# A decoder layer in one kernel: pacing of accumulating DMAs, new places for the next block's input, and 32-wide score products

## The chip, the cores and the metric

The kernel runs on one core of a Trainium2 chip. The metric is the device time of one launch in microseconds (us), the median of three runs. One further execution was taken by the hardware profiler; every duration below is from that one.

The names of the profile: PE is TensorE (matmuls), PEld its weight loads, DVE is VectorE, ACT is ScalarE, POOL is GpSimd, SP is SyncE, which here only issues DMAs. L12 is line 12 of the kernel before. In the changed kernel the lines stand a little lower: by 1 from L119, by 5 from L349, by 10 behind the scores and by 12 in FF2.

## What is computed

One inference step of a hybrid decoder layer, in float32, for one prompt of 2048 tokens and for 8 sequences of 8 sample tokens. Cut to what matters:

```python
proj = einsum('btd,dp->btp', x, w_in)                 # 1024 -> 3584
q, f_pre, i_val, g, gate_b, gate_c, h = split(proj)
qh, f, kh, vh = silu(q), gate(f_pre), 1 - f, i_val    # 4 heads of 128
S_t = diag(f_t) S_{t-1} + k_t outer v_t               # per head, 128x128
o_t = S_t^T q_t
o = rmsnorm(o) * onorm_g * silu(g)
yc = gate_b * conv3(gate_c * h)                       # causal, width 3
x = layer_norm(ALPHA * x + concat(o, yc) @ w_out)
hid = square(relu(x @ w_ff1))                         # 1024 -> 4096
x = layer_norm(ALPHA * x + hid @ w_ff2)               # 4096 -> 1024
```

The results are x for all tokens, the final states S, and the last two rows of the convolution's input.

## The kernel before

**Blocks and phases.** The prompt is worked in four blocks b = 0..3 of 512 tokens; block 1 carries the 64 sample tokens as well. A block has a phase m (the projections m1, m2, m3, the recurrence beside them, then the products with w_out) and a phase f (LayerNorm, FF1, FF2). The hidden width of 4096 falls into 8 chunks c of 512. The chunks come in two parts of four; each part runs its FF1 and then its FF2.

**Products.** A float32 product is three matmuls of rounded pieces: high by high, high by low, low by high (`mm3` L236 to L239, `mm3_on` L241 to L245, and `mm_pair` L247 for the sample tokens). So every operand is split in two: ACT writes the high piece, DVE subtracts it from the original and writes the low piece (`split` L161, where ACT's line is L162 and DVE's L163).

**Units of weights.** All weights, and the input x too, pass as a list of "units", each 128x1024 (512 KB). SP loads a unit into `st` (L180, three buffers); ACT makes `wh` (L201) and DVE `wl` (L208), four buffers each. `weights(i)` (L224) hands out unit i, and before that `ahead` (L215) issues the loads and splits up to three units further on. A unit of x has its own function: it splits `st` into the tile X (again L162 and L163). Since each engine works strictly in order, the place of a unit in the list is the place of its split in ACT's and DVE's queues, and of its load in SP's.

**Where the next block's x stands in the list.** While the list is built (L383), the units of x for block b+1 are put among the FF2 units of part 1: `X_PLACES` (L49) names the FF2 steps and the chunks after which the next one goes in. There are four such units, and a fifth one for the sample tokens before block 1.

**FF2 and FF1 by seven products.** FF2 of a part, and FF1 from chunk 2 on in blocks 1 to 3, use a scheme in the manner of Strassen: seven products (`PRODUCTS`, in the order T4, B11, B21, T2, T1, T3, B22) of sums of quarters in place of eight plain ones. Each FF2 step goes over the part's four chunks, 28 units of 12 matmuls (128x512) each. Before a unit `prepare` (L1197) splits a quarter of the hidden values into h (ACT L162) and l (DVE L163), three buffers each; it runs two units ahead, since the last two FF1 units each call it once. `sum_rows` (L1221) makes sums of hidden values on DVE, and at a step's end `add_to` (L1229) adds the step's two PSUM banks into the output tiles: two additions for some steps, four for T3.

**Sums of the weights.** The sums T1 to T4 of the quarters of w_ff2 (`T_b`) and of w_ff1 (`T_a`) are made once, in device memory, by DMAs that POOL issues: per chunk eight, half of them with an accumulating write (`make_sums` L340, issued at L345 and L347). The generator `making` makes the 64 for w_ff2 while block 0 is in its phase m, and `making1` the 48 for w_ff1 (chunks 2 to 7). In block 0's FF1, which is plain because T_a is not there yet, three `making1` steps follow each unit of part 0 and two each unit of part 1: 8 units of part 0 and 16 of part 1, so the 48 are used up by part 1. T_a is first read in block 1's FF1.

**The recurrence.** For a head (`head`, L564 to L698) the scores of 128 tokens by 128 tokens are put together by levels: on level `lev` the tokens are paired in neighbouring groups of L = 2^lev, keys from the one and queries from the other, and after each level `decay` multiplies the gates into q and k for the next. Levels 0 and 1 are sums made with a matrix of ones. On levels 2 to 6 PE multiplies keys by queries, for each of the four groups of 128 tokens of a block (L677). Level 4 and below use one product of 128x128 per group, level 5 two of 32x32, level 6 one of 64x64. On levels 2 to 4 DVE then takes the valid places out of PSUM by one predicated copy of 128 partitions by 256 elements (`place`, L597); on levels 5 and 6 there are plain copies of rectangles (L680). The steps of this generator are called between the units of m1, m2 and m3, so one level's matmuls stand as a short burst among the projections on PE, and its copies between the weight splits on DVE.

**Temporary tiles.** In phase f, `TMP` (L92) takes its tile from the three buffers tagged "h", which FF2's h uses too.

Of the kernel before, what the change touches and what calls it, by code (L numbers as in the profile page):

```python
# [9 lines left out]
F32 = mybir.dt.float32  # L10
# [3 lines left out]
ALU = mybir.AluOpType  # L14
# [31 lines left out]

SAMPLE = {"B21": (1, ((0, 1),)), "B11": (0, ((0, 1), (1, -1))), "T1": (0, ((1, 1),)), "B22": (1, ((1, 1),))}

X_PLACES = (("T3", 4), ("T3", 6), ("B22", 4), ("B22", 5), ("B22", 6))  # L49

QUARTER = {"B11": (0, 0), "B21": (1, 0), "B12": (0, 1), "B22": (1, 1)}

# [8 lines left out]
def hybrid_step(ctx, tc, a, o):  # L61
# [27 lines left out]

    def TMP():  # L90

        return S((P, 4, P)) if phase["in"] == "m" else new((P, 4, P), "h", 3, F32, phase["of"])  # L92

    def TOK(dt=F32):
        return new((P, D), "tok", 8, dt)
# [20 lines left out]
    small = cst.tile([P, 36], F32, name="small")  # L116
    lnb = cst.tile([P, 2, D], F32, name="lnb")
    nhalf = cst.tile([P, NH], F32, name="nhalf")
    halo = cst.tile([P, 4, 2], F32, name="halo")  # L119
    lw = cst.tile([P, 6, NH], F32, name="lw")  # L120
    lbl, onorm, convw = small[:, 0:4], small[:, 4:8], small[:, 8:20]
# [218 lines left out]
    def make_sums(at, cs):  # L340
        for to, of, acc in (("T1", "B11", False), ("T3", "B22", False), ("T1", "B12", True), ("T3", "B12", True),
                            ("T2", "T3", False), ("T2", "B11", True), ("T4", "T2", False), ("T4", "B21", True)):
            for c in cs:
                if acc:
                    g.dma_start(at(c, to), at(c, of), accum_op=ALU.add, max_dma_last_dim=4096)  # L345
                else:
                    g.dma_start(at(c, to), at(c, of), max_dma_last_dim=4096)  # L347
                yield

    making = make_sums(quarter2, range(NCH))  # L350
    making1 = make_sums(quarter1, range(NPLAIN, NCH))
# [46 lines left out]
    for b in range(NB):  # L398
# [165 lines left out]
        def head(h):  # L564
# [106 lines left out]
            for lev in range(2, 7):  # L671
                ps = PS((P, NC, P))
                L = 1 << lev
                for c in range(NC):

                    for x, y, w in (((0, 0, P),), ((0, 32, 32), (64, 96, 32)), ((0, 64, 64),))[max(lev - 4, 0)]:
                        te.matmul(ps[x:x + w, c, y:y + w], k3[:, c, x:x + w], q3[:, c, y:y + w], start=True, stop=True)  # L677
                if lev > 4:
                    for x in range(0, P, 2 * L):
                        v.tensor_copy(sc[x:x + L, :, x + L:x + 2 * L], ps[x:x + L, :, x + L:x + 2 * L])  # L680
                else:
                    place(lev, L, pairs(ps.rearrange("p c t -> p (c t)"), L)[:, :, 1, :])
                sample_scores(lev)
                decay(lev)
                yield
# [165 lines left out]
        for i, _ in enumerate(main()):  # L851
            rec_step()
            if b == 0 and i >= 6:
                if i == 6:

                    g.tensor_tensor(SM((P, 1)), ks[0][:, 0:1], fs[0][:, 0:1], ALU.add)
                next(making, 0)
                next(making, 0)
            if i >= 16 and i % (3 if samp else 4) == 0:
                rec_step()  # L860
            if i % 2 == 0:
                pump()
# [383 lines left out]
        for part, (ff1_units, ff2_units) in enumerate(pl["parts"]):  # L1246
            queue += [(step, c) for step, c, _ in ff2_units]
            for i, (step, c, u) in enumerate(ff1_units):
                if i >= len(ff1_units) - 2:
                    prepare()  # L1250
                if b == 0:
                    if i == 0:
                        for _ in making:
                            pass
                    ff1(step, weights(u), segs)
                    for _ in range(3 - part):
                        next(making1, 0)
                else:
                    ff1_product(step, c, weights(u))
            drain()  # L1260
# [19 lines left out]
            for n_, (step, c, u) in enumerate(ff2_units):  # L1280
# [15 lines left out]
                if first:  # L1296
                    banks[k] = [PS() for _ in range(2)]
                h, l = hid.pop((step, c))
                for p in range(2):
                    cs = slice(p * P, p * P + P)  # L1300
                    for q, (rh, rl) in enumerate(parts):
# [151 lines left out]
```

## Time and profile before

| | |
|---|---|
| median of three runs | 2425.33 us (2424.86 to 2428.46) |
| the profiled execution: its time | 2427.2 us |
| its span, first to last instruction | 2425.4 us |
| mean granted clock of PE | 0.993 |
| PE busy | 2369.6 us, 98% |
| DVE, ACT, POOL busy | 71%, 50%, 7% |
| moved by DMA | 412.40 MB, 170 GB/s on average |
| `T_b` and `T_a` DMAs of POOL, issue to landing (median) | 18 to 24 us |
| loads of `st` by SP, issue to landing (median) | 3.5 to 4.5 us |

A line of waits reads "engine tile line <- engine tile line that released it: us in all, times, longest". A line of the timeline reads "start, duration, engine, line, operation, tiles, shape, count", and in brackets the idle time before it and what ended it. A group of instructions reads "line engine op out<-in count | busy us, mean ns of one | idle before, releaser". "L245 <- l" is a matmul that waited for a low piece of hidden values, "L244 <- wl" one that waited for a low piece of weights, "L243 <- h" one that waited for a high piece of hidden values.

### The profile page before, as it was taken

To read this page: it belongs to the slowest core of one execution; us is meant where nothing else is said; L and a number is where in the kernel's file an instruction comes from. 1 tells how busy PE (TensorE), PEld (TensorE's weight loads), DVE (VectorE), ACT (ScalarE), POOL (GpSimd) and SP (SyncE) were. 2 spreads that over 40 slices of the span, in tenths; PEclk is the share of its full clock that TensorE was granted. 3 is DMA by queue.
4 is the path that set the end of the run, shared out by engine and by line. 5 is a ranking of instruction groups with operands and counts; after the bars stand their busy time and mean duration, and the time that the engine had idled before them with its cause. 6 is when DMAs were issued, how large, how long until landed. Compare 5 with 4: busy or idle time off the path is not lost. (4 is left out here: it accounts for less than half of the span.)

```text
span 2425.4 us, 34901 instructions
## 1 busy us (share of the span) xinstructions
PE 2369.6 (98%) x13596; PEld 2062.5 (85%) x13596; DVE 1729.7 (71%) x2651; ACT 1212.1 (50%) x1898; POOL 170.4 (7%) x208
## 2 busy tenths in 40 slices
PE   8999989999999999899999999999999999999998
PEld 7888977887989889779977888998987888998996
DVE  7756648258775677775687856888588965888678
ACT  5234535355423446556654324665665324575563
POOL 2220321000001110000000000000000001000001
PEclk9999999999999999999999999999999999999999
DMA  8996999346223644444544325465566225456563
GB/s 294 273 273 213 286 280 284 115 136 200 100 65 84 164 153 131 158 154 160 172 147 140 100 70 182 152 205 186 179 191 191 99 76 170 141 196 193 182 189 116
DMA packets 128229, 412.40 MB, mean 170 GB/s; under 512 B 13184, under 2 KB 17664, under 8 KB 128064
## 3 DMA queue, kind: packets, MB, share of 16 engines
q1 hardware_dynamic: 105904, 342.19, 43.3%
q0 software_dynamic: 22016, 67.71, 11.1%
q8 instruction: 107, 1.75, 0.3%
q14 instruction: 58, 0.48, 0.1%
q10 hardware_dynamic: 144, 0.26, 0.0%
HBM read 399.07 MB, written 69.77 MB: 193 GB/s over the span
## 5 line engine op out<-in xcount | busy, mean ns | idle before, releaser
L208 DVE TENSOR_TENSOR wl<-st,wh 128x1024 fp32r<-128x1024 f32 x568 | 692.5, 1220 | 218.7 <-ACT wh L201 217.5
L201 ACT ACTIVATE wh<-st 128x1024 fp32r<-128x1024 f32 x569 | 600.4, 1055 | 401.5 <-PE ps L245 118.7
L237 PE MATMUL ps<-X,wh 128*128 128x256 f32 (+2 forms) x1504 | 515.2, 343 | 8.5 <-ACT X L162 8.0
L239 PE MATMUL ps<-X,wl 128*128 128x256 f32 (+2 forms) x1504 | 505.7, 336 | 0.3 <-DVE wl L208 0.3
L238 PE MATMUL ps<-X,wh 128*128 128x256 f32 (+2 forms) x1504 | 505.7, 336 | 0.3 <-DVE X L163 0.3
L245 PE MATMUL ps<-wh,l 128*128 128x512 f32 x868 | 345.3, 398 | 10.7 <-DVE l L163 10.4
L243 PE MATMUL ps<-wh,h 128*128 128x512 f32 x868 | 341.3, 393 | 10.3 <-ACT h L162 10.3
L244 PE MATMUL ps<-wl,h 128*128 128x512 f32 x868 | 341.2, 393 | 5.5 <-DVE wl L208 5.4
L237 PEld LDWEIGHTS ps<-X,wh 128*128 128x128 f32 x1504 | 286.2, 190 | 37.7 <-ACT X L162 8.9
L239 PEld LDWEIGHTS ps<-X,wl 128*128 128x128 f32 x1504 | 285.8, 190 | 27.5 <-DVE wl L208 0.7
L238 PEld LDWEIGHTS ps<-X,wh 128*128 128x128 f32 x1504 | 286.2, 190 | 26.2 <-DVE X L163 1.4
L245 PEld LDWEIGHTS ps<-wh,l 128*128 128x128 f32 x868 | 164.3, 189 | 60.5 <-DVE l L163 26.9
L243 PEld LDWEIGHTS ps<-wh,h 128*128 128x128 f32 x868 | 164.7, 190 | 44.3 <-ACT h L162 11.8
L244 PEld LDWEIGHTS ps<-wl,h 128*128 128x128 f32 x868 | 164.3, 189 | 42.3 <-DVE wl L208 7.8
L163 DVE TENSOR_TENSOR l<-raw,h 128x512 fp32r<-128x512 f32 x217 | 148.2, 683 | 19.7 <-ACT h L162 19.7
L269 POOL TENSOR_TENSOR sm<-sm,nhalf 128x1 f32<-128x1 f32 (+1 forms) x34 | 35.1, 1033 | 1579.5 <-DVE sm L268 1533.3
L162 ACT ACTIVATE h<-raw 128x512 fp32r<-128x512 f32 x217 | 133.6, 616 | 4.4 <-DVE tok L1244 2.3
L245 PE MATMUL ps<-X,wl 128*128 128x256 f32 (+1 forms) x432 | 124.9, 289 | 0.0
L243 PE MATMUL ps<-X,wh 128*128 128x256 f32 (+1 forms) x432 | 124.9, 289 | 0.0
L244 PE MATMUL ps<-X,wh 128*128 128x256 f32 (+1 forms) x432 | 124.9, 289 | 0.0
L1134 DVE TENSOR_TENSOR raw<-raw,ps 128x256 f32<-128x256 f32 (+1 forms) x96 | 50.4, 551 | 85.1 <-PE ps L245 84.9
L237 PE MATMUL ps<-wh,X 128*128 128x512 f32 x256 | 104.1, 407 | 0.0
(256 smaller groups left out, 4122.1 us busy)
## 6 DMA issues: line engine op xcount, KB each, us to landing
st<-in_w_ff SPq DMA_DIRECT2D x231, 512.0 KB, 3.6
st<-T_b SPq DMA_DIRECT2D x124, 512.0 KB, 3.9
st<-in_w_in SPq DMA_DIRECT2D x110, 512.0 KB, 3.5
st<-T_a SPq DMA_DIRECT2D x72, 512.0 KB, 3.6
st<-in_w_out SPq DMA_DIRECT2D x56, 512.0 KB, 4.5
T_b<-in_w_ff POOLq DMA_DIRECT2D x48, 512.0 KB, 18.4
T_a<-in_w_ff POOLq DMA_DIRECT2D x36, 512.0 KB, 23.7
T_b<-T_b POOLq DMA_DIRECT2D x16, 512.0 KB, 19.1
```

Source lines behind the costliest of these rows:

```text
L162: s.activation(hi, src, AF.Copy)
L163: later.append(lambda: v.tensor_tensor(lo, src, hi.bitcast(F32), ALU.subtract))
L201: s.activation(wh, st, AF.Copy)
L208: v.tensor_tensor(wl, st, wh.bitcast(F32), ALU.subtract)
L237: te.matmul(out, lh, rh, start=first, stop=False)
L238: te.matmul(out, lh, rl, start=False, stop=False)
L239: te.matmul(out, ll, rh, start=False, stop=last)
L243: te.matmul(out, lh, rh, start=first, stop=False, skip_group_check=True)
L244: te.matmul(out, lh, rl, start=False, stop=False, skip_group_check=True)
L245: te.matmul(out, ll, rh, start=False, stop=last, skip_group_check=True)
L269: g.tensor_tensor(st[:n, 15:16], st[:n, 14:15], nhalf[:n, 0:1], ALU.pow)
L1134: v.tensor_tensor(z, z, ps, (ALU.add, ALU.subtract)[op - 2])
```

## The change

It has six parts.

1. **Places of x.** `X_PLACES` names other steps: one unit of x in each of T4, B11, B21 and T3 (after chunk 6), the fifth in B22; before, two stood in T3 and three in B22.
2. **TMP.** In phase f its tile has a tag of its own with two buffers.
3. **hold.** A one-column addition on POOL that reads the tile it is given; what POOL issues later waits until that tile is written.
4. **Scores of levels 2 to 4.** L is 4, 8 or 16, so every pair of groups lies within 32 neighbouring tokens. In place of one 128x128 product per group of 128 tokens there are four 32x32 products on its diagonal, 16 in a level in place of 4; and in place of one predicated copy of 128 partitions with 256 elements, four copies of 32 partitions with 64 elements.
5. **Pace of `making1`.** In block 0's FF1 one step per unit, each behind a `hold` on the hidden values of the chunk. Then one step at every fourth FF2 unit of block 0, behind a `hold` on h. What is left goes out in the phase m of block 1, one at every second unit. In numbers: 8 and 7 in part 0's FF1 and FF2, 16 and 7 in part 1's, the last 10 in block 1.
6. **prepare.** Its two early calls in FF1 come at the fifth and the fourth unit from the end, not at the last two.

```diff
@@ -46,7 +46,7 @@
 
 SAMPLE = {"B21": (1, ((0, 1),)), "B11": (0, ((0, 1), (1, -1))), "T1": (0, ((1, 1),)), "B22": (1, ((1, 1),))}
 
-X_PLACES = (("T3", 4), ("T3", 6), ("B22", 4), ("B22", 5), ("B22", 6))
+X_PLACES = (("T4", 6), ("B11", 6), ("B21", 6), ("T3", 6), ("B22", 5))
 
 QUARTER = {"B11": (0, 0), "B21": (1, 0), "B12": (0, 1), "B22": (1, 1)}
 
@@ -89,7 +89,7 @@
 
     def TMP():
 
-        return S((P, 4, P)) if phase["in"] == "m" else new((P, 4, P), "h", 3, F32, phase["of"])
+        return S((P, 4, P)) if phase["in"] == "m" else new((P, 4, P), "tmp", 2, F32, phase["of"])
 
     def TOK(dt=F32):
         return new((P, D), "tok", 8, dt)
@@ -116,6 +116,7 @@
     small = cst.tile([P, 36], F32, name="small")
     lnb = cst.tile([P, 2, D], F32, name="lnb")
     nhalf = cst.tile([P, NH], F32, name="nhalf")
+    tick = cst.tile([P, 1], F32, name="tick")
     halo = cst.tile([P, 4, 2], F32, name="halo")
     lw = cst.tile([P, 6, NH], F32, name="lw")
     lbl, onorm, convw = small[:, 0:4], small[:, 4:8], small[:, 8:20]
@@ -346,6 +347,10 @@
                 else:
                     g.dma_start(at(c, to), at(c, of), max_dma_last_dim=4096)
                 yield
+
+    def hold(x):
+
+        g.tensor_tensor(tick, x, x, ALU.add)
 
     making = make_sums(quarter2, range(NCH))
     making1 = make_sums(quarter1, range(NPLAIN, NCH))
@@ -673,13 +678,18 @@
                 L = 1 << lev
                 for c in range(NC):
 
-                    for x, y, w in (((0, 0, P),), ((0, 32, 32), (64, 96, 32)), ((0, 64, 64),))[max(lev - 4, 0)]:
+                    for x, y, w in ([(x, x, 32) for x in range(0, P, 32)], ((0, 32, 32), (64, 96, 32)), ((0, 64, 64),))[max(lev - 4, 0)]:
                         te.matmul(ps[x:x + w, c, y:y + w], k3[:, c, x:x + w], q3[:, c, y:y + w], start=True, stop=True)
                 if lev > 4:
                     for x in range(0, P, 2 * L):
                         v.tensor_copy(sc[x:x + L, :, x + L:x + 2 * L], ps[x:x + L, :, x + L:x + 2 * L])
                 else:
-                    place(lev, L, pairs(ps.rearrange("p c t -> p (c t)"), L)[:, :, 1, :])
+                    for x in range(0, P, 32):
+                        cs = slice(x, x + 32)
+                        m = masks[cs, lev, :].rearrange("p (c t) -> p c t", c=NC)[:, :, x // 2:x // 2 + 16]
+                        to_, of = (z[cs, :, cs].rearrange("p c (j r l) -> p c j r l", r=2, l=L)[:, :, :, 1, :]
+                                   for z in (sc, ps))
+                        v.copy_predicated(to_, m.rearrange("p c (j l) -> p c j l", l=L), of)
                 sample_scores(lev)
                 decay(lev)
                 yield
@@ -853,9 +863,11 @@
             if b == 0 and i >= 6:
                 if i == 6:
 
-                    g.tensor_tensor(SM((P, 1)), ks[0][:, 0:1], fs[0][:, 0:1], ALU.add)
+                    hold(ks[0][:, 0:1])
                 next(making, 0)
                 next(making, 0)
+            if b == 1 and i % 2 == 0:
+                next(making1, 0)
             if i >= 16 and i % (3 if samp else 4) == 0:
                 rec_step()
             if i % 2 == 0:
@@ -1246,15 +1258,15 @@
         for part, (ff1_units, ff2_units) in enumerate(pl["parts"]):
             queue += [(step, c) for step, c, _ in ff2_units]
             for i, (step, c, u) in enumerate(ff1_units):
-                if i >= len(ff1_units) - 2:
+                if len(ff1_units) - 5 <= i < len(ff1_units) - 3:
                     prepare()
                 if b == 0:
                     if i == 0:
                         for _ in making:
                             pass
                     ff1(step, weights(u), segs)
-                    for _ in range(3 - part):
-                        next(making1, 0)
+                    hold(values(c)[:, 0, 0, 0:1])
+                    next(making1, 0)
                 else:
                     ff1_product(step, c, weights(u))
             drain()
@@ -1296,6 +1308,9 @@
                 if first:
                     banks[k] = [PS() for _ in range(2)]
                 h, l = hid.pop((step, c))
+                if b == 0 and n_ % 4 == 0:
+                    hold(h[:, 0, 0:1].bitcast(F32))
+                    next(making1, 0)
                 for p in range(2):
                     cs = slice(p * P, p * P + P)
                     for q, (rh, rl) in enumerate(parts):
```

How this moves instructions shows at three places. **POOL's queue at the start of block 0's FF1** (`T_a` is the device memory that takes the sums, `in_w_ff` the weights), before:

```order
L347 DMA T_a_89<-in_w_ff 256x1x512
L347 DMA T_a_93<-in_w_ff 256x1x512
L347 DMA T_a_97<-in_w_ff 256x1x512
L347 DMA T_a_101<-in_w_ff 256x1x512
L347 DMA T_a_105<-in_w_ff 256x1x512
L347 DMA T_a_109<-in_w_ff 256x1x512
L347 DMA T_a_91<-in_w_ff 256x1x512
L347 DMA T_a_95<-in_w_ff 256x1x512
```

and with the change, from the second chunk of that FF1 to the first steps in FF2 (`raw` is a chunk's hidden values, `h` a high piece of them):

```order
L353 TENSOR_TENSOR tick<-raw_3090 128x1
L348 DMA T_a_106<-in_w_ff 256x1x512
L353 TENSOR_TENSOR tick<-raw_3090 128x1
L348 DMA T_a_110<-in_w_ff 256x1x512
L353 TENSOR_TENSOR tick<-raw_3090 128x1
L348 DMA T_a_92<-in_w_ff 256x1x512
L353 TENSOR_TENSOR tick<-raw_3090 128x1
L348 DMA T_a_96<-in_w_ff 256x1x512
L353 TENSOR_TENSOR tick<-h_3036 128x1
L348 DMA T_a_100<-in_w_ff 256x1x512
L353 TENSOR_TENSOR tick<-h_3288 128x1
L348 DMA T_a_104<-in_w_ff 256x1x512
```

The DMAs stood one behind the other; now each has a `tick` ahead of it, four times on the tile of one chunk and then, in FF2, once on each fourth h.

**DVE's queue at the end of step T3 in block 0's part 1** (`X` is the next block's input, `tok` an output tile, `ps` a PSUM bank), before:

```order
L163 TENSOR_TENSOR l_4779<-raw_4138,h_4778 128x512
L208 TENSOR_TENSOR wl_4815<-st_4796,wh_4798 128x1024
L163 TENSOR_TENSOR l_4801<-raw_3712,h_4800 128x512
L163 TENSOR_TENSOR X_4703<-st_4818,X_4701 128x2x512
L1229 TENSOR_TENSOR tok_1810<-tok_1810,ps_4376 128x512
L1229 TENSOR_TENSOR tok_1812<-tok_1812,ps_4377 128x512
L1229 TENSOR_TENSOR tok_1810<-tok_1810,ps_4376 128x512
L1229 TENSOR_TENSOR tok_1812<-tok_1812,ps_4377 128x512
L208 TENSOR_TENSOR wl_4845<-st_4822,wh_4824 128x1024
L163 TENSOR_TENSOR l_4827<-raw_3854,h_4826 128x512
L163 TENSOR_TENSOR X_4703<-st_4848,X_4701 128x2x512
L163 TENSOR_TENSOR l_4852<-raw_3996,h_4851 128x512
```

and with the change:

```order
L164 TENSOR_TENSOR l_4970<-raw_4182,h_4969 128x512
L209 TENSOR_TENSOR wl_5007<-st_4988,wh_4990 128x1024
L164 TENSOR_TENSOR l_4993<-raw_4332,h_4992 128x512
L209 TENSOR_TENSOR wl_5029<-st_5010,wh_5012 128x1024
L164 TENSOR_TENSOR l_5015<-raw_3898,h_5014 128x512
L209 TENSOR_TENSOR wl_5036<-st_5032,wh_5034 128x1024
L1241 TENSOR_TENSOR tok_1990<-tok_1990,ps_4579 128x512
L1241 TENSOR_TENSOR tok_1992<-tok_1992,ps_4580 128x512
L1241 TENSOR_TENSOR tok_1990<-tok_1990,ps_4579 128x512
L1241 TENSOR_TENSOR tok_1992<-tok_1992,ps_4580 128x512
L164 TENSOR_TENSOR tok_5040<-st_5038,tok_5040 128x8x64
```

Before, a split of X stood directly ahead of the step's four additions and another one soon behind them. Now the split of X that falls to this step comes seven rows earlier (in the row ahead of those shown), weight and hidden pieces stand between, and the small one for the sample tokens is behind the additions.

**DVE's queue at level 2 of the first head in block 0** (`ps_515` holds the level's products, `S_316` or `S_317` the scores), before:

```order
L208 TENSOR_TENSOR wl_491<-st_437,wh_439 128x1024
L597 COPY_PREDICATED S_316<-masks,ps_510 128x128x2 x2
L597 COPY_PREDICATED S_316<-masks,ps_515 128x64x4
L607 TENSOR_TENSOR S_237<-S_237,S_317 128x64x4
L608 TENSOR_TENSOR S_277<-S_277,S_317 128x64x4
L614 TENSOR_TENSOR S_317<-S_317 128x64
```

and with the change:

```order
L209 TENSOR_TENSOR wl_491<-st_437,wh_439 128x1024
L602 COPY_PREDICATED S_317<-masks,ps_510 128x128x2 x2
L692 COPY_PREDICATED S_317<-masks,ps_515 32x4x4x4 x4
L612 TENSOR_TENSOR S_238<-S_238,S_318 128x64x4
L613 TENSOR_TENSOR S_278<-S_278,S_318 128x64x4
L619 TENSOR_TENSOR S_318<-S_318 128x64
```

One copy has become four at the same place, and nothing else in the row has moved.

## The prediction

> **What bounds the kernel now.** I read the totals first, then what TensorE (PE) waited for, then the stretches where those waits lie. The page's totals and its line of DMA shares (40 slices of 60.6 us):
>
> ```profile
> PE 2369.6 (98%) x13596; PEld 2062.5 (85%) x13596; DVE 1729.7 (71%) x2651; ACT 1212.1 (50%) x1898; POOL 170.4 (7%) x208
> DMA  8996999346223644444544325465566225456563
> ```
>
> PE is the bound, nearly everywhere. A change can win only by less PE time or by the few per cent in which PE stands still. DMA is full until about 420 us, then half idle. The waits of PE by line, with total us, how many and the longest:
>
> ```profile
> PE ps L245 <- DVE l L163: 10.4, 16, 1.3
> PE ps L243 <- ACT h L162: 10.3, 2, 6.9
> PE ps L248 <- DVE hp L163: 8.9, 3, 3.3
> PE ps L237 <- ACT X L162: 8.0, 2, 6.4
> PE ps L244 <- DVE wl L208: 5.4, 4, 2.1
> ```
>
> These are 43.0 us, a ceiling for all edits that only remove waits. Where they lie shows in stretches (length, PE busy and matmuls, granted clock, DMA share, GB/s):
>
> ```profile
> 340.00:420.00 80.00, 68.87 (x278) 0.96 0.98 288
> 500.00:580.00 80.00, 80.00 (x350) 1.00 0.53 165
> 583.00:590.00 7.00, 4.92 (x14) 0.78 0.55 160
> 1260.00:1290.00 30.00, 25.70 (x107) 1.00 0.63 195
> 1840.00:1846.00 6.00, 3.92 (x15) 1.00 0.64 190
> ```
>
> The second row is FF2 undisturbed: 80.00/350 = 0.2286 us from one 128x512 matmul to the next. By that pace 340–420 lost 80.00 − 278 × 0.2286 = 16.5 us, at 0.98 of DMA. The last three rows, the ends of blocks 0, 1 and 2, lost 3.8 + 5.5 + 2.6 = 11.9 us by the same sum.
>
> All sums are made against the profiled execution's own 2427.2 us (span 2425.4); it is 1.9 above the median of 2425.33, to which the same differences are applied. A difference of about 0.2% (4.9 us) is what a measurement of this kernel can tell from none.
>
> **Part A, the sums of w_ff1 are paced.** Before, block 0's FF1 lets POOL issue all 48 T_a DMAs at once, as its queue allows. The DMA view of 300–424 us (queue, packets, MB, share of 16 engines; median us to landing):
>
> ```profile
> q0 software_dynamic: 7015, 16.47, 57.9%
> q1 hardware_dynamic: 5044, 18.37, 41.1%
> st<-T_b SPq DMA_DIRECT2D x16, 512.0 KB, 6.8
> ```
>
> POOL's traffic takes more than the weights'. What that does to PE at the seam from FF1 to FF2 (issue on SP, landing seen by ACT, PE's wait), and the same two steps in block 1, where no T_a is made:
>
> ```profile
> 333.00 0.36 SPq L180 DMA_DIRECT2D st<-T_b  x1
> 344.83 1.06 ACT L201 ACTIVATE wh<-st 128x1024 fp32r<-128x1024 f32 x1 [9.43 <-DMA st<-T_b]
> 345.79 0.61 ACT L162 ACTIVATE h<-raw 128x512 fp32r<-128x512 f32 x1
> 346.46 0.80 PE L243 MATMUL ps<-wh,h 128*128 128x512 f32 x1 [6.92 <-ACT h L162]
> 994.85 0.38 SPq L180 DMA_DIRECT2D st<-T_b  x1
> 1000.65 1.06 ACT L201 ACTIVATE wh<-st 128x1024 fp32r<-128x1024 f32 x1 [3.27 <-DMA st<-T_b]
> ```
>
> The unit needs 344.83 − 333.00 = 11.83 us in block 0 and 5.80 in block 1. h (L162) stands behind that wh in ACT's queue, so a landing 6.0 us earlier takes the wait from 6.92 to 0.9. After the change 8 T_a DMAs remain in part 0's FF1, four per chunk in a clump, because only a chunk's first tick waits for new data. The second clump starts within some 20 us of the seam, so I do not take block 1's landing whole: 1.9 us remain (an estimate: a sixth of the 6.0 is not won). The rest of 340–420 is l behind late units; with one DMA per four units it goes, save the step-end wait of an undisturbed block
>
> ```profile
> 1683.83 0.51 PE L245 MATMUL ps<-wh,l 128*128 128x512 f32 x1 [0.54 <-DVE l L163]
> ```
>
> so 0.5, and 0.6 for a clump that still meets a landing. A: 16.5 − 1.9 − 0.5 − 0.6 = **−13.5**; bounds −9 (landing halfway, half of the small waits stay) and −16. Nothing is late behind it: T_a is first read in block 1's FF1, which ends at the 994.85 above, and the last ten DMAs go out in block 1's m phase, where the DMA line shows 2 to 6 tenths. Behind a waiting tick on POOL stand its own DMA, the later ones and the powers of the norms, none of which is due in FF1; and a later write of the tile that a tick reads (by DVE or ACT) must wait for POOL, whose 7% leave it free.
>
> **Part B, the next block's x.** The end of T3 in block 0, DVE and PE:
>
> ```profile
> 583.16 2.47 DVE L1229 TENSOR_TENSOR tok<-tok,ps 128x512 f32<-128x512 f32 x4
> 585.55 1.22 DVE L208 TENSOR_TENSOR wl<-st,wh 128x1024 fp32r<-128x1024 f32 x1
> 586.69 0.68 DVE L163 TENSOR_TENSOR l<-raw,h 128x512 fp32r<-128x512 f32 x1
> 586.82 0.70 PE L244 MATMUL ps<-wl,h 128*128 128x512 f32 x1 [2.08 <-DVE wl L208]
> 1823.62 1.21 DVE L163 TENSOR_TENSOR X<-st,X 128x1024 fp32r<-128x1024 f32 x1
> ```
>
> Four additions, 2.47 us in a row, come to a DVE that has just been set back by x splits (1.21 each, and the wait for ACT's half before them): the next wl is 2.08 us late. With one split per step the four additions remain, and with them the 0.54 seen above, 0.7 with the clock's recovery: 3 × 0.7 = 2.1 stay. Of block 1's 5.5 one wait for hp, which no x place touches, is in the window; 8.9 less two of 3.3 is 2.3, and half of it may close by DVE's earlier progress: 1.1 stays. New: the first split is queued where FF2 of part 1 begins, ahead of the third h and l, and ACT's half may not write while FF1 still reads its buffer. The cover is two units of 12 matmuls (5.5 us) that are already split, against 1.21 for x, 1.22 for a wl and 0.68 for an l on DVE; I put 0.5 for each of three blocks, 1.5. Their loads move on SP with them, each a place among weight loads that run three units ahead with DMA at 0.53: covered. B: −11.9 + 2.1 + 1.1 + 1.5 = **−7.2**, bounds −10 and −3 (a step-end wait of 2 us at another step each time).
>
> **Part C, scores on PE.** Levels 2 to 4, 4 heads, 4 blocks: 48 bursts. Such a burst before, and level 5, which already has 32-wide products (8 of them):
>
> ```profile
> 45.99 1.05 PE L677 MATMUL ps<-S,S 128*128 128x128 f32 x8
> 46.80 0.48 PE L237 MATMUL ps<-X,wh 128*128 128x512 f32 x1
> 47.11 0.39 PE L238 MATMUL ps<-X,wh 128*128 128x512 f32 x1
> ...
> 72.92 0.39 PE L239 MATMUL ps<-wh,X 128*128 128x512 f32 x1
> 73.23 0.45 PE L677 MATMUL ps<-S,S 128*32 128x32 f32 x16
> 73.61 0.50 PE L237 MATMUL ps<-wh,X 128*128 128x512 f32 x1
> 73.94 0.39 PE L238 MATMUL ps<-wl,X 128*128 128x512 f32 x1
> ...
> L677 PE MATMUL ps<-S,S 128*32 128x32 f32 x256 | 7.1, 199 | 0.0
> ```
>
> The wide burst costs 46.80 − 45.99 = 0.81, and the next interval is 0.31, 0.08 above the pace: 0.89 us. Level 5 costs 0.31 − 0.23 ahead, 0.38, and 0.33 − 0.23 behind: 0.56 us. Its 16 records, 0.199 each, start (0.45 − 0.199)/15 = 16.7 ns apart. The new burst has 32. Lower bound: four column strips run as the two of level 5 do and nothing is added, 0.56. Upper: the added 16 records at 16.7 ns, 0.83. I take 0.70, in the middle, since twice the strips may overlap but the starts still queue. C: 48 × (0.70 − 0.89) = **−9.1**; bounds −15.8 and −2.9. The Trainium skill, "TensorEngine Tiling (Array Packing)", section Key Properties, says that a change of tiling mode drains the array, where different tiles run in parallel; the 0.08 ahead and 0.10 behind level 5's burst agree in kind, and are in the sum already.
>
> **Part D, the copies on DVE.** One predicated copy of 128x256 becomes four of 32 partitions with 64 elements. The nearest rows, and DVE's fullest stretch (PE, PEld, DVE, ACT, POOL):
>
> ```profile
> L597 DVE COPY_PREDICATED S<-masks,ps 128x256 f32<-128x256 uint8 x96 | 56.1, 584 | 44.3 <-PE ps L677 21.3 <-PE ps L639 20.4
> L590 DVE COPY_PREDICATED sq<-masks,ps x12: 175/211/225, 623.5 to 724.4; 64x32 f32<-64x32 uint8 x12
> L680 DVE COPY S<-ps 32x128 f32<-32x128 f32 x32 | 9.0, 282 | 12.9 <-PE ps L677 12.7
> 1878.60:1939.20 60.60, 60.60 (x317) 50.59 (x316) 56.46 (x114) 21.60 (x33) 3.46 (x5) 1.00 0.28 96
> ```
>
> A quarter lies between 0.211 (32 elements) and 0.282 (128): 0.23. Four make 0.92 against 0.584, +0.34 per level, 16 us of DVE in all. In the fullest stretch, m1 of block 3, DVE has 4.14 us left with seven bursts, 0.59 each, and PE stood nowhere: the excess is covered, barely. D: **+2.0** (an eighth of it shows), bounds 0 and +8 (half). Free are the tmp tag (it removes waits for h's buffers, and none of PE's waits names it), the tick tile, and prepare three units earlier: its split (0.61 on ACT, 0.68 on DVE, both above) finds engines at 50% and 71%; without that cover it costs a wait of that length, twice per part.
>
> Sum: −13.5 − 7.2 − 9.1 + 2.0 = **−27.8**: 2399.4 for the profiled execution, **2397.5** for the median.
>
> **The rivals.** (1) The traffic only moves: the 40 T_a DMAs that leave meet FF2 of block 0 and block 1's m phase, and A is halved, +6.8: 2404. For it: 512 KB that are read, added and written as before, a full DMA up to 420 us. Against: 3 to 6 tenths from 424 us to the end of block 0.
> (2) The ticks hold nothing (their data are ready when POOL comes by), so the DMAs go in as thick a clump: A is 0, +13.5: 2411. Against: one per unit where POOL had two or three.
> (3) Small products do not overlap. A record of the new burst then takes 25 ns, an estimate midway between 16.7 and twice that (level 5's in pairs): 0.56 + 32 × 0.025 − 16 × 0.0167 = 1.09 us, +0.20 over the wide burst, C = +9.6: 2416. Against: level 5's 16.7 is a measured mean. The Trainium skill, "TensorE: Matmul & The Clock Gate", section "Wait — 56ns, not 53.3ns?", gives about 25 ns as the least start-to-start time however small the product; by that rule the time is that of this rival, and the trace's 16.7 ns disagrees.
> (4) Slower: a quarter costs as much as a whole copy, since length is not what a copy pays for. Then each level adds 3 × 0.584 = 1.75 us to DVE, 0.59 of it covered, and wl (L208), queued behind, makes PE wait 1.16 us at each of 48: D = +56, 2451. It decides from 1.2 us extra per level (0.59 + 29.8/48), some 0.45 us a quarter. Against: L590's 0.211.
>
> **How the numbers follow.** Forecast 0.70, rival 1 0.12, rival 2 0.05, rival 3 0.04, rivals 2 and 3 together 0.05 (2411 + 18.7 = 2430, within 0.2%), rival 4 0.04. The range: all four lower bounds together give 2425.3 − 16 − 10 − 15.8 = 2384; upwards it takes in rivals 1 and 2 to 2414. Faster by over 0.2%: 0.70 + 0.12 + 0.05 + 0.04 = 0.91, of which I give 0.03 to several upper bounds meeting, 0.01 of it within 0.2% and 0.02 beyond: 0.88. Within 0.2%: 0.05 + 0.01 = 0.06. Slower: 0.04 + 0.02 = 0.06.
>
> **What would show it.** A: PE busy over 79 of 80 us in the stretch after the seam, the wait for h under 2.5 us, q0's share before 424 us halved. B: no wait for wl above 1 us at the ends of blocks 0, 1 and 2. C: bursts at 0.70 from interval to interval, their records under 17 ns apart. D: quarter copies at 0.23, m1 of block 3 without PE waits. Wrong would be: a quarter at 0.45 or more, T_a DMAs still at 60% of DMA at the seam, or x splits with new waits at the ends of T4, B11 and B21.

## The result, and the profile of the changed kernel

The changed kernel takes 2408.38 us (median of four runs, 2406.01 to 2443.95) against 2426.89 for the kernel before (four runs, 2424.86 to 2429.91). The ratio is 0.9919, 95% interval 0.99 to 0.9939: faster by some 20 us, where 27.8 were forecast. The execution of 2443.95 us was the profiled one; its granted clock was 0.945 from end to end, the comparison leaves it out, and the profile shown here is a second one of the same kernel, from experiment 1 (2405.18 us, span 2403.3, clock 0.995).

Its totals and DMA shares, as those of the kernel before were shown:

```profile
PE 2349.5 (98%) x14748; PEld 2032.2 (85%) x14748; DVE 1757.6 (73%) x2795; ACT 1209.5 (50%) x1898; POOL 188.7 (8%) x246
DMA  8996577887523743444553325565565325466563
```

PE has 20.1 us less to do and DVE 27.9 more. Slices 5 to 7 of DMA, full before, are down to 5 to 7 tenths, and slices 8 to 10, which had 3, 4 and 6, have 8, 8 and 7. What PE waited for:

```profile
PE ps L246 <- DVE l L164: 14.9, 20, 1.3
PE ps L238 <- ACT X L163: 8.2, 2, 6.6
PE ps L249 <- DVE hp L164: 7.5, 3, 3.3
PE ps L238 <- DVE S L602: 3.8, 3, 1.4
PE ps L244 <- ACT h L163: 3.1, 2, 2.8
PE ps L682 <- ACT tok L505: 2.7, 2, 1.4
```

(hp are the pieces of the sample tokens' hidden values.) The wait for wl above 1 us is gone and h's longest fell from 6.9 to 2.8 (that one is block 1's). But l rose from 10.4 to 14.9, and two waits are new or nearly so, L238 on S (0.5 before) and L682 on tok. Together PE waits about 42 us, hardly less than the 43.0 before. The stretches show where (PE busy and matmuls, clock, DMA share, GB/s); the last three are the ends of blocks 0, 1 and 2:

```profile
340.00:420.00 80.00, 79.46 (x346) 1.00 0.76 224
500.00:580.00 80.00, 74.80 (x310) 0.98 0.79 233
565.00:580.00 15.00, 14.18 (x63) 1.00 0.79 261
1238.00:1268.00 30.00, 28.64 (x126) 1.00 0.56 172
1816.00:1830.00 14.00, 13.28 (x59) 1.00 0.77 220
```

By the pace of 0.2286 us, 340–420 lost 0.9 us in place of 16.5, and the ends of the blocks 0.6, 1.2 and 0.5 in place of 3.8, 5.5 and 2.6. Both stretches that the forecast spoke of are mended. The queue of the accumulating DMAs, which took 57.9% of DMA's time in 300–424 us, is down to less than half of that there:

```profile
q0 software_dynamic: 2659, 7.77, 26.3%
```

But 500–580, undisturbed before, now loses 80.00 − 310 × 0.2286 = 9.1 us. What comes late there, by ACT's rows, is the loads:

```profile
527.18 1.06 ACT L202 ACTIVATE wh<-st 128x1024 fp32r<-128x1024 f32 x1 [3.73 <-DMA st<-in_w_ff]
538.40 1.06 ACT L202 ACTIVATE wh<-st 128x1024 fp32r<-128x1024 f32 x1 [4.02 <-DMA st<-T_b]
```

The score bursts, a narrow one between two steady stretches, and the groups of the quarter copies, of the whole copies that are left, and of the narrow products:

```profile
54.61 0.39 PE L240 MATMUL ps<-X,wl 128*128 128x512 f32 x1
54.92 0.46 PE L682 MATMUL ps<-S,S 128*32 128x32 f32 x32
55.31 0.50 PE L238 MATMUL ps<-wh,X 128*128 128x512 f32 x1
55.65 0.39 PE L239 MATMUL ps<-wl,X 128*128 128x512 f32 x1
...
L692 DVE COPY_PREDICATED S<-masks,ps 32x64 f32<-32x64 uint8 x192 | 43.2, 225 | 14.3 <-PE ps L682 9.7
L602 DVE COPY_PREDICATED S<-masks,ps 128x256 f32<-128x256 uint8 x48 | 35.2, 734 | 11.6 <-PE ps L644 10.6
L682 PE MATMUL ps<-S,S 128*32 128x32 f32 x1792 | 28.2, 199 | 0.0
```

32 records begin and end within 0.46 us, where the 16 of level 5 took 0.45: the added products cost next to nothing. The single starts in the trace say why. They come in fours, 5 to 8 ns apart, and from the second four on each follows some 32 ns after the one before; level 5's come in twos, and each two also follows after some 32 ns. Both bursts have eight such steps, so a third and a fourth strip in a step are free.

The burst costs 0.31 − 0.23 ahead, 0.39, and 0.34 − 0.23 behind: 0.58 us, just above the forecast's lower bound of 0.56, against 0.89. A quarter copy is 0.225, as forecast (0.23). But the whole copy that four of them replace was cheaper than the 0.584 of the forecast. That was the mean of 96 copies (56.1 us), and the 48 of them that the change leaves alone take 0.734, 35.2 us; so the 48 of levels 2 to 4 took (56.1 − 35.2)/48 = 0.435. A level now costs DVE 0.90 − 0.435 = 0.47 us more, 22 us in all, and not 0.34 and 16.

Both kernels run the same projections and the same FF matmuls in the same order, so the start of one and the same matmul can be compared. The lead of the changed kernel, worked out from the two traces:

```
place in the changed kernel             its lead, us   step
start                                    0.5
end of block 0's m1 to m3      160 us    4.6          +4.1  scores
block 0, first seam            330       3.5          -1.1  a wait at 173 us
block 0, FF2 of part 0 done    415      18.4         +14.9  the paced sums, and prepare
block 0, FF2 of part 1         555      10.4          -7.9  late loads at 510 to 545
block 0, end                   595      14.0          +3.6  x at T3's end
block 1, recurrence done       720      17.9          +3.9  scores
block 1, last seam             1215     15.1          -2.8  hp and a slower clock behind it
block 1, end                   1300     20.7          +5.6  x at T3's end
block 2, m1                    1343     22.1          +1.4  scores
                               1360     19.7          -2.4  PE waits for the copies
                               1440     21.7          +2.0  scores
block 2, FF2 of part 1         1790     18.9          -2.8  a wait for l at 1599 us (1.0), x splits at other steps
block 2, end                   1835     21.2          +2.3  x at T3's end
block 3, m1                    1900     22.5          +1.3  scores
                               1920     20.2          -2.3  PE waits for the copies
                               1960     22.1          +1.9  scores, and so to the end
```

So 15 us from the sums (prepare's share included), 11.5 from x and 14.6 from the scores were won, and some 19 given back, most of it at places where PE had not stood before.

### The profile page after: what moved, and what is told of

Same layout as the page of the kernel before. It is cut to its first block, busy times and chain, and to the rows that moved or that the text cites. A ratio compares the mean times of both kernels' runs of the same rounds, so it can differ in the third digit from the quotient of the medians.

```text
span 2442.1 us, 37413 instructions
## 1 busy us (share of the span) xinstructions
PE 2391.1 (98%) x14748; PEld 2044.8 (84%) x14748; DVE 1757.8 (72%) x2795; ACT 1209.8 (50%) x1898; POOL 191.1 (8%) x246
## 4 chain that ended last, share of the span: by engine, by line
PE 49%; DVE 5%; issue 1%; DMA 1%; ACT 0%; DVEq 0%; ACTq 0%
PE ps L246 10%; PE ps L244 9%; PE ps L245 9%; PE ps L238 6%; PE ps L240 6%; PE ps L239 6%; DVE wl L209 1%; PE ps L249 1%; DMA st<-in_w_ff 1%; PE ps L250 1%; PE ps L682 1%; DVE tok L1241 0%; DVE S L602 0%; DVE l L164 0%; DVE sm L265 0%
## 5 line engine op out<-in xcount | busy, mean ns | idle before, releaser
L238 PE MATMUL ps<-X,wh 128*128 128x256 f32 (+2 forms) x1504 | 524.7, 349 | 9.6 <-ACT X L163 8.1
L239 PE MATMUL ps<-X,wh 128*128 128x256 f32 (+2 forms) x1504 | 514.7, 342 | 0.3 <-DVE X L164 0.3
L240 PE MATMUL ps<-X,wl 128*128 128x256 f32 (+2 forms) x1504 | 514.4, 342 | 0.0
L238 PEld LDWEIGHTS ps<-X,wh 128*128 128x128 f32 x1504 | 288.1, 192 | 45.2 <-ACT X L163 9.1
L238 PE MATMUL ps<-wh,X 128*128 128x512 f32 x256 | 106.4, 416 | 2.8 <-DVE S L602 2.8
```

The source lines that it names most:

```text
L238: te.matmul(out, lh, rh, start=first, stop=False)
L239: te.matmul(out, lh, rl, start=False, stop=False)
L240: te.matmul(out, ll, rh, start=False, stop=last)
```

## The experiments

The theory, begun on that first profiled execution and completed with this one: the narrow products were cheaper than forecast, and part of what the three edits won is given back, 8 us because the T_a DMAs and the x loads now meet in block 0's last FF2, and 5 to 10 because PE, with shorter bursts, catches up with a DVE that has more to copy. The rival: the terms are the forecast's, and something else in the change costs the difference. All medians stand beside the kernel before on the same chip; "gain" is the difference from that. A gain's interval reaches 3 to 4 us to either side, so a smaller difference between two rows is read together with its place in the traces.

| | kernel | median | before | gain | ratio, interval |
|---|---|---|---|---|---|
| 1 | changed | 2405.52 | 2427.43 | 21.9 | 0.9908 (0.9893 to 0.9923) |
| 2 | old scores | 2409.83 | 2427.43 | 17.6 | 0.9925 (0.991 to 0.994) |
| 3 | old pace | 2414.72 | 2427.43 | 12.7 | 0.9944 (0.9929 to 0.9958) |
| 4 | old x places | 2410.00 | 2427.43 | 17.4 | 0.9922 (0.9905 to 0.9938) |
| 5 | calm last FF2 | 2400.47 | 2426.38 | 25.9 | 0.989 (0.9876 to 0.9903) |
| 6 | wide products, quarter copies | 2414.03 | 2426.38 | 12.4 | 0.995 (0.9936 to 0.9963) |
| 7 | no holds | 2408.32 | 2426.38 | 18.1 | 0.9922 (0.9908 to 0.9937) |
| 8 | old prepare and TMP | 2412.14 | 2426.38 | 14.2 | 0.9933 (0.992 to 0.9947) |
| 9 | calm, halves | 2400.57 | 2427.96 | 27.4 | 0.9891 (0.9877 to 0.9906) |
| 10 | calm, old x places | 2406.45 | 2427.96 | 21.5 | 0.9913 (0.9897 to 0.993) |
| 11 | old prepare | 2409.16 | 2427.96 | 18.8 | 0.9923 (0.9908 to 0.9938) |
| 12 | calm, mixed | 2392.77 | 2427.33 | 34.6 | 0.9854 (0.9837 to 0.987) |

**Experiment 1** is the changed kernel, unedited.

> The changed kernel once more, for a profile at full clock. First theory: the narrow score burst costs about 0.57 us from interval to interval (16 more records add nothing, since the four column strips run together), so C gives 48 x 0.32 = 15 us, and about 24 of the 28.4 us that the two stretches of stalls held are removed, but new waits of about 20 us come in elsewhere: at 560 to 582 us in block 0's last FF2 steps, where the T_a DMAs now meet x loads, and in the m phases of blocks 1 to 3. Rival: the burst costs the forecast 0.70 at full clock, C gives 9, and A and B gave together 9 to 11 less the copies. Time under both 2406 to 2409; a burst of 0.57 or of 0.70 and PE waits of about 40 us or of about 25 tell them apart.

The burst is 0.58 and the waits are 42 us, as shown above: the first theory on both counts.

**Experiment 2** takes the old scores, products and copies.

```diff
-for x, y, w in ([(x, x, 32) for x in range(0, P, 32)], ...
+for x, y, w in (((0, 0, P),), ...
-for x in range(0, P, 32):
-    ...
-    v.copy_predicated(to_, m.rearrange("p c (j l) -> p c j l", l=L), of)
+place(lev, L, pairs(ps.rearrange("p c t -> p (c t)"), L)[:, :, 1, :])
```

> The changed kernel with the old scores (one 128x128 product per group and one whole copy on levels 2 to 4); everything else as changed. First theory: 15 us of PE come back and the waits behind the score copies (about 6 us at 746, 1386 and 1946 us in the changed kernel) go: +9, about 2417. Rival (burst 0.70, no waits due to the copies): +9 of PE and nothing off, also 2417, but then the waits for the recurrence's tiles at those three places stay. A third case, that the copies cost nothing at all and the burst 0.57: +15, 2423.

It loses 4.3 us, less than every case named, though PE pays 48 × 0.31 = 14.9 us more. So, by this difference, the copies with all that hangs on them cost about 10 us in the changed kernel. The lead's table places some 6 of them (1.1 at 173 us, 2.4 in block 2, 2.3 in block 3); where the rest goes is not shown. The place of block 2 where the lead shrank, in the changed kernel (waits in the brackets, and the stretch) and then in this one:

```profile
1346.65 0.50 PE L238 MATMUL ps<-wh,X 128*128 128x512 f32 x1 [1.41 <-DVE S L602]
1348.97 1.07 PE L682 MATMUL ps<-S,S 128*64 128x64 f32 x40 [1.36 <-ACT tok L505]
1338.00:1358.00 20.00, 17.24 (x140) 1.00 0.34 106
```

```profile
1338.00:1358.00 20.00, 20.00 (x121) 1.00 0.31 106
```

With the old scores PE does not stand there at all. In the changed kernel it waits for PSUM banks that DVE and ACT have yet to empty (L602 and L505 both read `ps`); DVE has LayerNorm's last steps for the block before in the same stretch. The Trainium skill, "TensorEngine Tiling (Array Packing)", section PSUM Bottleneck, says that a tiled product speeds up TensorE but not the emptying of PSUM, so that the copies may become the bound; these rows agree.

**Experiment 3** takes the old pace of the w_ff1 sums.

```diff
-hold(values(c)[:, 0, 0, 0:1])
-next(making1, 0)
+for _ in range(3 - part):
+    next(making1, 0)
 ...
-if b == 0 and n_ % 4 == 0:
-    hold(h[:, 0, 0:1].bitcast(F32))
-    next(making1, 0)
 ...
-if b == 1 and i % 2 == 0:
-    next(making1, 0)
```

> The changed kernel with the old pace of the w_ff1 sums (three and two DMAs per FF1 unit, no hold, none later). First theory: the 16.5 us lost at 340 to 420 us come back, less what of it prepare's new place covers (1 to 3), and the new waits at 560 to 582 us (some 5 us) go: +9, about 2417. Rival, by the prediction's own size for A: +13.5, 2421; and a third, that the waits at 560 to 582 are due to the x loads and stay: +15, 2422.

```profile
340.00:420.00 80.00, 71.66 (x289) 0.98 0.99 288
500.00:580.00 80.00, 79.84 (x349) 1.00 0.61 188
```

9.2 us slower, the first theory's number. 340–420 loses 13.9 us again, and 500–580 none, with the new x places still in.

**Experiment 4** takes the old x places.

```diff
-X_PLACES = (("T4", 6), ("B11", 6), ("B21", 6), ("T3", 6), ("B22", 5))
+X_PLACES = (("T3", 4), ("T3", 6), ("B22", 4), ("B22", 5), ("B22", 6))
```

> The changed kernel with the old places of x. First theory: the three late weight pieces at the ends of blocks 0, 1 and 2 return (11.9 us), while the waits of about 1 us behind x splits elsewhere and most of those at 560 to 582 us go (6 to 8): +4 to +6, about 2413. Rival, by the prediction's size for B: +7.2, 2415. If the new places give back all that they take: no difference, 2408.

4.5 us slower. Against the changed kernel, matmul by matmul, it leads by 7.9 us after 510 to 545 us, and gives 6.7 back at the end of block 0, where the kernel before lost 3.6 by the same comparison. So neither edit alone makes PE stand at 510 to 545. Two waits of the changed kernel in blocks 1 and 2, which this one does not have, are the price of the new places there:

```profile
1188.91 0.50 PE L249 MATMUL ps<-wh,hp 128*128 128x512 f32 x1 [0.80 <-DVE hp L164]
1767.27 0.50 PE L246 MATMUL ps<-wh,l 128*128 128x512 f32 x1 [1.33 <-DVE l L164]
```

**Experiment 5** keeps both, and takes the sums out of block 0's last FF2.

```diff
-if b == 0 and n_ % 4 == 0:
+if b == 0 and part == 0 and n_ % 4 == 0:
 ...
-if b == 1 and i % 2 == 0:
+if b == 1:
     next(making1, 0)
```

> The changed kernel, but block 0's last FF2 (part 1) issues none of the w_ff1 sums; its 7 go out in block 1's m phase, one at every unit there. Theory: the late loads at 510 to 550 us of the changed kernel are a meeting of two edits, T_a DMAs and x loads in the same FF2 (each of the two undone alone removed them): PE stands there 7 to 8 us less, 2398. Rival: the clumps of four at the end of FF1 are enough (eight T_a DMAs go out in the 25 us ahead of that FF2): 2 to 3 us less, 2403. If the m phase of block 1 then pays the same: 2406.

```profile
500.00:580.00 80.00, 78.77 (x355) 1.00 0.70 207
```

PE stands 1.2 us in this stretch in place of 5.2 (of the 355 matmuls, some 30 are already narrower ones of the next block). The sums' share of DMA's time in 500–550 us and the median landing of a T_b load, in the changed kernel, and then the landing here, where no sums go out:

```profile
q0 software_dynamic: 1061, 2.06, 27.1%
st<-T_b SPq DMA_DIRECT2D x9, 512.0 KB, 4.8
```

```profile
st<-T_b SPq DMA_DIRECT2D x11, 512.0 KB, 4.4
```

Matmul by matmul it gains 7.4 us on the changed kernel between 500 and 555 us; 2.8 of it were lost again at 1350 us in the profiled execution, where the clock fell behind the waits of experiment 2. The median is 5.1 us lower and its gain 4.0 larger, less than the 7 to 8 of the theory and more than the rival's 2 to 3. The place shows the meeting: without these seven DMAs the waits go, and the clumps ahead of this FF2, which are still there, are not what makes PE wait.

**Experiment 6** puts the old products under the new copies.

```diff
-for x, y, w in ([(x, x, 32) for x in range(0, P, 32)], ...
+for x, y, w in (((0, 0, P),), ...
```

> The changed kernel with the old wide products but the new quarter copies: D without C. Theory: the copies cost time because PE, with its shorter bursts, catches up with a DVE that has 0.45 us more per level to do; with the wide bursts the waits at 1346 and 1907 us shrink but do not go, +3 over the kernel with wide products and whole copies, 2413. Rival 4's kind: each level's longer copies delay the weight pieces by themselves, +7 or more: 2417. If DVE's spare time covers them all: 2410.

```profile
1353.39 1.77 PE L682 MATMUL ps<-S,S 128*64 128x64 f32 x16 [1.35 <-ACT tok L505]
1915.83 1.77 PE L682 MATMUL ps<-S,S 128*64 128x64 f32 x16 [1.34 <-ACT tok L505]
```

Its gain is 5.2 below experiment 2's (4.2 by the bare medians), between the two cases. One wait of 1.35 is left of the two at each place. So the copies cost some 5 us under wide products and, by experiments 1 and 2, some 10 under narrow ones. That the shorter PE makes this difference is what the second wait, there only with narrow products, speaks for; the times alone are too near their noise to show it.

**Experiment 7** drops the holds, not the number of DMAs per unit.

```diff
-hold(values(c)[:, 0, 0, 0:1])
 next(making1, 0)
 ...
-hold(h[:, 0, 0:1].bitcast(F32))
 next(making1, 0)
```

> The changed kernel without the holds; the number of w_ff1 DMAs per unit is as changed. Theory: it is the ticks that pace the DMAs; without them POOL runs ahead to the limit of its eight DMAs in flight and the 340 to 420 us lose what they lost before (14 to 15 us), while the waits at 510 to 550 us go (7 to 8): +7, 2413. Rival 2 of the prediction (the ticks hold nothing): no difference, 2406.

```profile
340.00:420.00 80.00, 73.48 (x304) 0.98 0.82 249
500.00:580.00 80.00, 78.87 (x342) 1.00 0.61 187
```

POOL runs ahead: 340–420 loses 10.5 us, 500–580 1.8. The theory had 7 us, and the time shows 2.8 (3.8 by the gains, with intervals that overlap). The ticks do pace, and the place says so more plainly than the time, because the loss in the one stretch and the gain in the other nearly cancel.

**Experiments 8 and 11** put prepare back to the last two FF1 units, experiment 8 TMP as well.

```diff
-if len(ff1_units) - 5 <= i < len(ff1_units) - 3:
+if i >= len(ff1_units) - 2:
 ...
-new((P, 4, P), "tmp", 2, F32, phase["of"])
+new((P, 4, P), "h", 3, F32, phase["of"])
```

> The changed kernel with prepare back at FF1's last two units and TMP back among h's buffers. By the prediction these two are free: 2405 to 2407. Rival: the early h and l cover part of the seam between FF1 and FF2 (the wait for h at block 1's seam was 3.4 us before and 2.8 in the changed kernel; the three single undos add up to 18 of 22 us): +2 to +4, 2409.

> The changed kernel with prepare back at FF1's last two units, TMP as changed. Theory: of the 7 us that the two edits together were worth, all is prepare's: the wait for h at block 0's seam of 2.2 us with its slower clock, and the one in block 1: 2410 to 2412. Rival: TMP's own buffers carry a part (its tile is free earlier at the step ends of block 1): 2407 and under.

The seam of block 0 in experiment 8 and in experiment 11; the changed kernel has no wait for h there:

```profile
341.19 0.50 PE L244 MATMUL ps<-wh,h 128*128 128x512 f32 x1 [2.23 <-ACT h L163]
```

```profile
343.70 0.50 PE L244 MATMUL ps<-wh,h 128*128 128x512 f32 x1 [1.30 <-ACT h L163]
```

By the starts of the matmuls this seam costs 3.7 us more than the changed kernel's in experiment 8 and 1.6 in experiment 11. By the gains the early prepare is worth 3.1 (experiment 11, between its two cases) or, with TMP, 7.7 (experiment 8, more than either case named); but 11's runs spread over 10 us and its profiled execution lost 6.9 us at 174 to 178 us, long before any prepare. TMP's share stays open.

**Experiment 9** tries a middle way on the calm kernel, the one of experiment 5: 64-wide products, two copies of 64 partitions (the masks' slice is widened with them).

```diff
-for x, y, w in ([(x, x, 32) for x in range(0, P, 32)], ...
+for x, y, w in ([(x, x, 64) for x in range(0, P, 64)], ...
-for x in range(0, P, 32):
-    cs = slice(x, x + 32)
+for x in range(0, P, 64):
+    cs = slice(x, x + 64)
```

> The calm kernel (block 0's last FF2 without sums), with two 64x64 products per group in place of four 32x32 and two copies of 64 partitions in place of four of 32. Theory: a level costs DVE about 0.6 us in place of 0.9 (whole copy 0.44), so the waits at 172, 707, 1347 and 1908 us shrink by 4 to 8 us; two strips of 64 columns run together as the four of 32 did, so a burst costs about 0.67 in place of 0.58, 4 us over 48 bursts: 26 to 30 us under the kernel before, 2397 to 2400. Rival: products of 64 do not run together: 16 records at the 58 ns of level 6, bursts of 1.1 us, +25: 2420.

```profile
45.89 0.39 PE L644 MATMUL ps<-S,ones 128*128 128x512 f32 x1
46.21 0.69 PE L682 MATMUL ps<-S,S 128*64 128x64 f32 x16
46.83 0.50 PE L238 MATMUL ps<-X,wh 128*128 128x512 f32 x1
47.16 0.39 PE L239 MATMUL ps<-X,wh 128*128 128x512 f32 x1
...
L692 DVE COPY_PREDICATED S<-masks,ps 64x128 f32<-64x128 uint8 x96 | 28.2, 294 | 18.3 <-PE ps L682 15.6
1342.15 1.17 PE L682 MATMUL ps<-S,S 128*64 128x64 f32 x24 [0.21 <-ACT tok L505]
```

The stall is down to 0.21 us, but a burst costs 0.32 − 0.23 ahead, 0.62, and 0.33 − 0.23 behind, 0.81 us and not 0.67: its gain is 1.5 above experiment 5's, no difference. Against 32-wide products, 48 × (0.81 − 0.58) = 11 us of PE were paid to save the waits.

**Experiment 10** is the calm kernel with the old x places (the diffs of 4 and 5).

> The calm kernel with the old places of x: B by itself, where the T_a DMAs no longer meet the x loads. Theory: without that meeting the new places are worth what the three late weight pieces cost less 3 to 4 us of new small waits in blocks 1 and 2, so the old places cost 8 to 10 here, against 4.5 in the changed kernel: 2409. Rival (the new places are worth the same with and without): +4.5, 2405.

```profile
PE ps L245 <- DVE wl L209: 6.8, 4, 2.5
```

The late wl are back, 6.8 us in four waits. The gain is 4.4 smaller than experiment 5's (6.0 by the bare medians), the rival's number and below the theory's 8 to 10: the new places are worth 4 to 6 us with or without the meeting, since blocks 1 and 2 wait a little at other steps.

**Experiment 12** uses both findings: the calm kernel, with 64-wide products and two copies only in heads 0 and 1 of blocks 2 and 3, where the quarter copies made PE wait.

```diff
+wd = 64 if b >= 2 and h < 2 else 32
-for x, y, w in ([(x, x, 32) for x in range(0, P, 32)], ...
+for x, y, w in ([(x, x, wd) for x in range(0, P, wd)], ...
-for x in range(0, P, 32):
-    cs = slice(x, x + 32)
+for x in range(0, P, wd):
+    cs = slice(x, x + wd)
```

> The calm kernel, with 64-wide products and two copies only where the quarter copies made PE wait: heads 0 and 1 of blocks 2 and 3 (12 bursts); everywhere else four 32-wide products and four copies. Theory: the stalls at 1340 and 1902 us (2.8 us each and up to 2.5 of slower clock) go as with 64 everywhere, and 36 bursts cost 0.58 in place of 0.81, 8 us, less 1 to 2 us of waits at 172 and 700 us: 33 us under the kernel before, 2393 to 2396. Rival: DVE's longer work in the rest of these blocks' heads makes PE wait a little later instead: 2398 to 2400, as both of its parents.

The two places in it, and the first of them in the calm kernel with narrow products everywhere:

```profile
1330.00:1350.00 20.00, 19.76 (x148) 1.00 0.32 106
1890.00:1910.00 20.00, 19.77 (x149) 1.00 0.34 106
```

```profile
1330.00:1350.00 20.00, 17.25 (x128) 0.83 0.33 106
```

2392.77 us, ratio 0.9854 (0.9837 to 0.987): 34.6 under the kernel before, the fastest here, and as the theory had it.

## Why the prediction came out as it did

The direction and the range were right; the gain is some 20 us, not 27.8, and that is no single step. Of the signs that the prediction named, the stretch behind the seam, the queue's share, the late wl and the quarter copy came as forecast; the burst (0.58), the waits in m1 of block 3 and the new waits behind x splits did not.

- **What bounds the kernel**: right. PE's waits and PE's own time were the two places to win.
- **A, −13.5**: right where it was put. Experiment 5 against experiment 3 differs by the pace alone: 25.9 − 12.7 = 13.2.
- **"Nothing is late behind it"**: wrong, and of the steps this one failed outright. Pacing moves the DMAs to block 0's last FF2, where part B had just put more loads; each term was worked out with the other one absent. The meeting cost 7 to 8 us at its place, 4 to 5 in the medians. Rival 1 had the mechanism ("the traffic only moves", 6.8 us), not the partner.
- **B, −7.2**: mechanism right, size 4 to 6 (experiments 4, 5 and 10). The wl waits went; smaller ones came at other steps (0.80 us of hp in block 1, 1.3 of l in block 2).
- **C, −9.1**: mis-sized. The burst is 0.58, not 0.70, so C is 48 × 0.31 = −14.9. Level 5 in the trace before had two strips in use, and its starts come in twos some 32 ns apart; the mean of 16.7 ns hides that. The step "the starts still queue" failed: they queue within a strip and hardly across strips, and the middle between the bounds had no row for it.
- **D, +2.0**: mis-sized, 5 under wide products and 10 under narrow. The quarter copy's duration was right, but the whole copy it was set against took 0.435 and not 0.584, which is a mean over two kinds: the excess is 0.47 us a level, not 0.34. And the cover was read from a stretch with the old, slower PE; with C in, PE arrives earlier at the same DVE queue. By the prediction's own row, an estimate: of the 4.14 us that DVE had left, seven shorter bursts take 7 × 0.31 = 2.2, and the 1.9 that remain are less than the 7 × 0.47 = 3.3 of the copies. And it is PSUM banks that come late, not wl as rival 4 had it.
- **prepare at nothing**: it covers 1.6 to 3.7 us of the seam, which the forecast had left in A's residue as 1.9.
- **Rivals**: 2 fell (experiment 7), 3 fell with the burst's 0.58 (16.7 was a mean, and within a strip the starts are 32 ns apart, but the strips do overlap), 4 was right in kind (DVE bounds part of the gain) and far off in size.

C and D together come out at −4.3 (experiment 2), not far from the forecast's −9.1 + 2.0 = −7.1. That is luck: C is off by 5.8 us to the one side and D by some 8 to the other.

With A −13.2, the meeting +4, B −4.4, scores and copies −4.3 and prepare −3.1, the sum is −21, against 21.9 in experiment 1. This leaves TMP at nothing; with experiment 8's 7.7 for prepare and TMP it would be −25.6. Each part is a difference of two gains whose intervals reach 3 to 4 us to either side, so this is agreement, not proof of each.

## What to carry to other kernels

Terms that are right one by one need not add: ask of every pair of edits whether one moves work into the stretch in which the other spends its slack. When PE is made shorter, cost the engines that feed it and empty its banks against the new, shorter PE, not against the old trace. And where an edit wins in some blocks and loses in others, apply it only where it wins, as experiment 12 did.

## What the runs showed of the hardware

- Products that use different strips of 32 columns run together: 32 records over four strips take 0.46 us, 16 over two 0.45. Their starts are 5 to 8 ns apart across strips, and a strip's turn comes again after some 32 ns. Two strips of 64 take 0.69 us for 16 records, with a turn of some 58 ns. The Trainium skill, "TensorE: Matmul & The Clock Gate", section "Wait — 56ns, not 53.3ns?", has about 25 ns as the least time from start to start. The turns of 32 ns keep to it; from strip to strip, these runs show a third of it or less.
- Waits of 1.4 us may cost more than they last. At the same two waits in block 2, the granted clock stayed at 1.00 in one execution (experiment 1; the second wait lies in its first row) and fell to 0.57 in another (experiment 8; the second wait lies in its row), and the other one lost 2.5 us more there:

```profile
1346.00:1352.00 6.00, 3.99 (x52) 1.00 0.60 184
1352.00:1358.00 6.00, 6.00 (x57) 1.00 0.25 81
```

```profile
1352.00:1358.00 6.00, 4.64 (x48) 0.57 0.59 223
```

So one profiled execution can be a few us better or worse than the next at places that an edit does not touch. The Trainium skill, "TensorE: Matmul & The Clock Gate", section "Part 1: The HAM clock gate", says that the clock is set by a free-running window of about 3.4 us, so that the moment of a change depends on where in a window the first matmul lands. That the same waits end differently in two executions agrees with such a window; that two waits of 1.4 us, with matmuls between them, can be enough is what experiment 8's trace shows.
